# A two-layer hybrid decoder step: the same instructions, ordered by another model of the engines

## The chip, the cores and the metric

The kernel runs on one core of a Trainium2 chip. Its engines work side by side, each from a queue of its own that is fixed when the program is built: TensorE (PE in the profile) multiplies matrices, VectorE (DVE), ScalarE (ACT) and GpSimd (POOL) do the element-wise work, and SyncE (SP) starts most of the transfers. The metric is the device time of one execution in microseconds (us), the median of several runs.

## The reference

One inference step of a decoder trunk with two layers, for 288 tokens: a new sequence of 256 and 8 sequences of 4 sample tokens with states that are carried on. Each layer feeds x to one wide input projection; its columns go to three token mixers, and the results are merged by gates:

```python
proj = jnp.einsum('btd,de->bte', x, w_in)
(a_qkv, a_z, a_beta, a_decay, r_q, r_k, r_v, r_g,
 m_q, m_k, m_v, m_o, m_i, m_f, gates) = jnp.split(proj, split_at, axis=-1)
...
# A gated DeltaNet (causal conv, chunked triangular solve), B retention, C mLSTM
...
x = LN(alpha * x + mix)
x = LN(alpha * x + squared_relu_mlp(x))
```

D_MODEL is 1024, the MLP's inner width 4096, each mixer has four heads of 128. The mixers' states, old and new, are read and written.

## The kernel before, in words

Tokens lie along the free dimension (288 columns), features along the partitions, in 8 slices of 128. All weights are streamed once, in blocks of 512 KB (`wr`, 4 buffers), in the order of SyncE's queue. As products are taken in a split form of fp32, ScalarE rounds each block to a high part (L358, `wh` or `bh`) and VectorE subtracts it for the low part (L360, `wl` or `bl`). One output tile of 128 features is 24 matmuls: for each of 8 slices high by XH, high by XL, low by XH (L367 to L369; L375 to L377 where three tiles go side by side; L504 where a "filler" issues them in pieces between other work). XH and XL are the high and low part of x, made in the same way.

A layer goes through these stages. Convolution and gates: the projections of the DeltaNet come first, VectorE runs the short convolution (L610), and a chain of small 4-row operations makes the gates' sums (L646 to L720). It ends in `dr` (L720), which TensorE needs for `dec` (L724). Then comes a block of small TensorE work: `colp` and `cols` (L733 to L751), transposes `tp` (L409), masks `rm` and `rms` (L809 to L819), Gram products G (L844) and KQ (L801, L854). Between its steps the source calls the filler, which issues projections of the retention mixer (rk, rv, rg; tiles `pj`). Retention's output OR is normalised (`finish`, L965 to L975, with an rsqrt of eleven small VectorE steps, L382 to L393) and transposed (L982). Then follow W and the triangular solve, the products with the states (`kSs`, `qSs`, `rcr`, `mcr`, Xs at L1213, which reads R from L1196), the state's updates (GpSimd scales at L937), the projections of the three branches (`pg`, `br`) and `wo`.

LayerNorm (L1290 to L1381) stands behind `wo` and behind the MLP. To gain time it takes the next matrix product over the sums before they are normalised: three tiles `g1` are multiplied by the raw values, and corrected later by mean, rstd and two columns `wgb` (L1376 to L1380, tile `u`). p1 and p2 (L1339, L1340) are the mean and the square sum, as matmuls by ones. VectorE makes mean and variance (L1345 to L1347), y minus mean (L1355), with ScalarE's Ln and Exp rstd (L1349 to L1353), then for each slice y times rstd (L1359); ScalarE makes XH of it (L1361), VectorE or ScalarE XF (L1365 or L1363), VectorE XL = XF - XH (L1367). The first tiles of the MLP, `f1`, need XH and XL of every slice. After the second LayerNorm it is the next layer's `pj`.

The order in each engine's queue is set by the tile layer: it takes the instructions in the source's order, with what they depend on, and a model of the engines by which it decides which ready instruction goes next into which queue. Two helpers tie single instructions to others (`tc.issue_after`, in `paced` and `Stream.get`), and the constants FILL_* and AHEAD_* say how many matmuls the fillers issue and how many blocks are fetched early. Semaphores and the buffers of the pools are put in afterwards.

## Time and profile before

| | us |
| --- | --- |
| median of three runs | 1285.8 (1285.58 to 1287.79) |
| the profiled execution | 1285.11 |
| its span | 1283.3 |
| TensorE busy | 1201.7 (94%) |
| VectorE busy | 909.0 (71%) |
| ScalarE busy | 597.1 (47%) |
| GpSimd busy | 126.6 (10%) |

The granted clock of TensorE was 0.97 on the mean. A share of busy time is a mean over stages that are limited by different things; so each stage is read by its own window, and each wait by what ended it. In the rows, "[4.80 <-DVE dr L720]" means that the engine had been idle for 4.80 us, and that the end of VectorE's instruction of line 720, which wrote `dr`, let it go on. Buffer numbers are left out in names.

### The profile page before, as it was taken

What the parts mean: (1) busy time and instruction counts of PE and PEld (TensorE: products, weight loads), DVE (VectorE), ACT (ScalarE), POOL (GpSimd) and SP (SyncE); (2) the same over time, 40 slices, a digit from 0 to 9 for tenths busy, and PEclk for the clock granted to TensorE, in tenths of its full rate; (3) what the DMA queues carried; (4) which work ended last, traced back from release to release, by engine and by line L of the source; (5) the groups of instructions that cost most, each with busy time, mean ns of one, the idle gap of its engine ahead of it and who ended that gap; (6) DMA issues with size and microseconds to landing.
All of it is one profiled execution on the core that took longest, in us unless ns stands there. A gap on an engine that the chain in (4) does not pass through costs nothing.

```text
span 1283.3 us, 22945 instructions
## 1 busy us (share of the span) xinstructions
PE 1201.7 (94%) x9210; PEld 1169.4 (91%) x9210; DVE 909.0 (71%) x1617; ACT 597.1 (47%) x1006; POOL 126.6 (10%) x107
## 2 busy tenths in 40 slices
PE   9989899889999999999997988998899998999995
PEld 8978799789999899999996987997799998999995
DVE  6988846596558974566899877556856688645665
ACT  5645324433445653455584532453334566534532
POOL 1113400330000000000000413004200000000000
PEclk9989999889999999999998998998899998999998
DMA  8443624348554465555714454253575543655551
GB/s 311 124 146 107 214 85 152 124 181 243 166 167 123 142 181 164 168 168 162 245 57 133 119 176 154 90 182 140 169 211 164 165 156 94 193 166 165 164 165 38
DMA packets 69794, 201.27 MB, mean 157 GB/s; under 512 B 11688, under 2 KB 22232, under 8 KB 69560
## 3 DMA queue, kind: packets, MB, share of 16 engines
q1 hardware_dynamic: 68744, 197.64, 49.1%
q0 software_dynamic: 944, 2.17, 0.5%
q8 instruction: 72, 1.18, 0.4%
q14 instruction: 34, 0.28, 0.1%
HBM read 180.62 MB, written 17.03 MB: 154 GB/s over the span
## 4 chain that ended last, share of the span: by engine, by line
PE 71%; DVE 18%; DMA 4%; ACT 3%; issue 3%; SPq 1%; DVEq 0%; ACTq 0%
PE f L369 9%; PE f L367 9%; PE f L368 9%; PE pj L504 6%; DVE wl L360 5%; PE pg L367 4%; PE pg L368 4%; PE pg L369 4%; PE pj L369 2%; PE pj L368 2%; PE pj L367 2%; PE br L367 2%; PE br L368 2%; PE br L369 2%; DMA wr<-in_w_ff 1%
## 5 line engine op out<-in xcount | busy, mean ns | idle before, releaser
L360 DVE TENSOR_TENSOR wl<-wr,wh 128x1024 fp32r<-128x1024 f32 x292 | 370.8, 1272 | 182.2 <-ACT wh L358 175.3
L358 ACT CAST wh<-wr 128x1024 fp32r<-128x1024 f32 x292 | 306.2, 1050 | 398.6 <-PE f L368 96.0
L369 PE MATMUL f<-fh,wl 128*128 128x288 f32 x512 | 151.2, 295 | 0.0
L367 PE MATMUL f<-fh,wh 128*128 128x288 f32 x512 | 151.1, 295 | 0.0
L368 PE MATMUL f<-fl,wh 128*128 128x288 f32 x512 | 151.0, 295 | 0.0
L369 PE MATMUL f<-XH,wl 128*128 128x288 f32 x416 | 122.5, 295 | 1.3 <-DVE wl L360 1.3
L368 PE MATMUL f<-XL,wh 128*128 128x288 f32 x416 | 123.1, 296 | 0.0
L367 PE MATMUL f<-XH,wh 128*128 128x288 f32 x416 | 122.9, 296 | 0.0
L367 PE MATMUL pg<-XH,wh 128*128 128x288 f32 x384 | 116.6, 304 | 0.0
L368 PE MATMUL pg<-XL,wh 128*128 128x288 f32 x384 | 114.9, 299 | 0.0
L369 PE MATMUL pg<-XH,wl 128*128 128x288 f32 x384 | 114.3, 298 | 0.0
L369 PE MATMUL pj<-XH,wl 128*128 128x288 f32 x352 | 107.2, 306 | 6.6 <-DVE wl L360 6.6
L367 PE MATMUL pj<-XH,wh 128*128 128x288 f32 x352 | 106.9, 304 | 1.7 <-ACT CV L596 1.7
L368 PE MATMUL pj<-XL,wh 128*128 128x288 f32 x352 | 106.1, 302 | 0.0
L504 PE MATMUL pj<-XH,wh 128*128 128x288 f32 x320 | 99.9, 312 | 0.0
L504 PE MATMUL pj<-XL,wh 128*128 128x288 f32 x320 | 98.1, 306 | 0.0
L504 PE MATMUL pj<-XH,wl 128*128 128x288 f32 x320 | 97.8, 306 | 0.0
L369 PEld LDWEIGHTS f<-fh,wl 128*128 128x128 f32 x512 | 96.3, 188 | 0.1
L367 PEld LDWEIGHTS f<-fh,wh 128*128 128x128 f32 x512 | 96.2, 188 | 0.2
L368 PEld LDWEIGHTS f<-fl,wh 128*128 128x128 f32 x512 | 96.2, 188 | 0.1
L369 PEld LDWEIGHTS f<-XH,wl 128*128 128x128 f32 x416 | 78.4, 189 | 1.8 <-DVE wl L360 1.7
L367 PEld LDWEIGHTS f<-XH,wh 128*128 128x128 f32 x416 | 78.6, 189 | 0.0
(508 smaller groups left out, 2887.9 us busy)
## 6 DMA issues: line engine op xcount, KB each, us to landing
wr<-in_w_in SPq DMA_DIRECT2D x141, 512.0 KB
wr<-in_w_ff SPq DMA_DIRECT2D x128, 512.0 KB
wr<-in_w_out SPq DMA_DIRECT2D x16, 512.0 KB
S<-in_state_ml_C SPq DMA_DIRECT2D x8, 516.0 KB
S<-in_state_ret_R SPq DMA_DIRECT2D x8, 512.0 KB
out_s_R<-S SPq DMA_DIRECT2D x8, 512.0 KB
S<-in_state_dn_S SPq DMA_DIRECT2D x8, 512.0 KB
out_s_S<-S SPq DMA_DIRECT2D x8, 512.0 KB
```

The costliest lines, as they stand in the source:

```text
L358: S.copy(hi[:, k, :], r[:, k, :])
L360: V.tensor_tensor(lo[:, k, :], r[:, k, :], hi[:, k, :].bitcast(F32), op=ALU.subtract)
L367: PE.matmul(ps, hi[:, k, :], xh[k], start=start and k == 0, stop=False)
L368: PE.matmul(ps, hi[:, k, :], xl[k], start=False, stop=False)
L369: PE.matmul(ps, lo[:, k, :], xh[k], start=False, stop=stop and k == KT - 1)
L504: ins = PE.matmul(self.ps[:, :T], self.w[i // 2][:, k, :], (xh, xl, xh)[i][k], start=self.k == 0, stop=self.k == 23)
```

## The change

One argument is added where the program is built. With it the tile layer orders the instructions by a simulation of the engines' timeline in place of its default model. The source of the computation, the pools and the constants are the same, and so are the instructions: 8574 matmuls, 447 transfers and four loads of activation tables in both.

```diff
-    with tile.TileContext(nc) as tc:
+    with tile.TileContext(nc, schedule_with_timeline_sim=True) as tc:
         tile_trunk(tc, a)
```

What moves is the order in the queues, in both layers alike. Three places follow; the numbers in names tell tiles apart.

TensorE's queue around `dec` in layer 1, before. `dec`, `colp` and `cols` stand between matmuls of the filler for rk (`pj_912`):

```order
L504 MATMUL pj_912<-XH_85,wh_908 128x288
L504 MATMUL pj_912<-XL_86,wh_908 128x288
L724 MATMUL dec_869<-dr_845,ones 128x64
L733 MATMUL colp_883<-ident,RS_72_649 128x128 x2
L733 MATMUL colp_883<-ident,RS_73_650 128x128 x2
L743 MATMUL cols_899<-ident,rep_900 128x128
L504 MATMUL pj_912<-XH_85,wl_909 128x288
L504 MATMUL pj_912<-XH_85,wh_908 128x288
```

The same place after; `pj_1247` is the last tile of rv, CO are the convolved values, and `csd` their sample columns:

```order
L504 MATMUL pj_1247<-XH_85,wl_1244 128x288
L724 MATMUL dec_869<-dr_845,ones 128x64
L733 MATMUL colp_883<-ident,RS_72_649 128x128 x2
L733 MATMUL colp_883<-ident,RS_73_650 128x128 x2
L743 MATMUL cols_899<-ident,rep_900 128x128
L409 MATMUL tp_983<-ident,CO_362 128x128 x4
L409 MATMUL tp_989<-ident,CO_362 128x128 x4
L409 MATMUL tp_995<-ident,csd_38_382 128x128
L409 MATMUL tp_1055<-ident,CO_461 128x128 x4
L743 MATMUL cols_899<-ident,rep_903 128x128
```

All tiles of rk and rv have moved ahead of `dec`, which goes from row 429 of TensorE's queue to row 556, and the block behind it stands without projection matmuls up to G.

VectorE's queue in the LayerNorm after `wo` of layer 1, before; `yo` is y, `wl_4887` a split of a weight block, and `u_4855` the correction of the first g1 tile:

```order
L360 TENSOR_TENSOR wl_4887<-wr_4884,wh_4886 128x1024
L1352 TENSOR_TENSOR rstd_4812<-rstd_4812,Cb_4382 128x288
L1376 COPY wgb_4853<-g_750_4731 128x2
L1353 SCALAR_TENSOR_TENSOR rstd_4812<-rstd_4812,Cb_4382 128x288
L1378 SCALAR_TENSOR_TENSOR u_4855<-sd_4383,wgb_4853,g_750_4731 128x288
L1359 TENSOR_TENSOR yo_4380<-yo_4380,rstd_4812 128x288 x2
L1365 TENSOR_SCALAR XF_4820<-yo_4380,vec 128x288 x2
L1367 TENSOR_TENSOR XL_4459<-XF_4820,XH_4458 128x288 x2
```

And after:

```order
L1378 SCALAR_TENSOR_TENSOR u_4867<-sd_4383,wgb_4865,g_752_4733 128x288
L1352 TENSOR_TENSOR rstd_4812<-rstd_4812,Cb_4382 128x288
L1353 SCALAR_TENSOR_TENSOR rstd_4812<-rstd_4812,Cb_4382 128x288
L360 TENSOR_TENSOR wl_4998<-wr_4995,wh_4997 128x1024
L360 TENSOR_TENSOR wl_5034<-wr_5031,wh_5033 128x1024
L1359 TENSOR_TENSOR yo_4380<-yo_4380,rstd_4812 128x288 x4
L1359 TENSOR_TENSOR yo_4381<-yo_4381,rstd_4812 128x288 x4
L1379 TENSOR_TENSOR u_4855<-u_4855,rstd_4812 128x288
L1379 TENSOR_TENSOR u_4861<-u_4861,rstd_4812 128x288
L1379 TENSOR_TENSOR u_4867<-u_4867,rstd_4812 128x288
L1365 TENSOR_SCALAR XF_4820<-yo_4380,vec 128x288 x3
L1365 TENSOR_SCALAR XF_4820<-yo_4381,vec 128x288 x2
```

The eight L1367 (XL) stand behind these rows, where before the first two of them came after two L1359. On TensorE p1 and p2 of this LayerNorm have moved as well, to the end of the g1 tiles:

```order
L376 MATMUL g_752_4733<-XL_4459,bh_4715 128x290
L377 MATMUL g_752_4733<-XH_4458,bl_4716 128x290
L1339 MATMUL p_728_4659<-sd_4383,ones 128x288
L1340 MATMUL p_729_4660<-sqs_4384,ones 128x288
L375 MATMUL f_777_4890<-XH_4458,bh_4721 128x288
L375 MATMUL f_778_4891<-XH_4458,bh_4727 128x288
```

Before, 48 matmuls of g1 stood between p2 and f. In the LayerNorm between the layers L1352 and L1353 moved behind the `wgb` and L1378 of the g1 tiles, and again all of L1359 ahead of the first XL.

VectorE's queue ahead of OR in layer 1, before, where `fr` is the result of the rsqrt, and two splits stand between its steps and the multiply:

```order
L360 TENSOR_TENSOR wl_1902<-wr_1899,wh_1901 128x1024
L392 TENSOR_TENSOR rsu_262_1736<-rsu_262_1736,rst_261_1727 128x8
L548 SCALAR_TENSOR_TENSOR ZG_1718<-ZG_1718,pj_1792 128x288
L393 SCALAR_TENSOR_TENSOR fr_259_1725<-rsu_262_1736,rsy_260_1726 128x8
L386 TENSOR_SCALAR rst_283_1871<-rst_283_1871 128x1
L360 TENSOR_TENSOR wl_1976<-wr_1973,wh_1975 128x1024
L974 TENSOR_SCALAR fr_259_1725<-fr_259_1725 128x8
L387 TENSOR_TENSOR rsy_282_1870<-rsy_282_1870,rst_283_1871 128x1
L975 TENSOR_TENSOR OR_1477<-OR_1477,fr_259_1725 128x1024
```

And after:

```order
L392 TENSOR_TENSOR rsu_262_1736<-rsu_262_1736,rst_261_1727 128x8
L393 SCALAR_TENSOR_TENSOR fr_259_1725<-rsu_262_1736,rsy_260_1726 128x8
L974 TENSOR_SCALAR fr_259_1725<-fr_259_1725 128x8
L948 SCALAR_TENSOR_TENSOR S_1551<-S_1551,up_1668 128x2x128 x2
L1045 TENSOR_TENSOR OR_1477<-smp_1581,ros_1583 128x128
L975 TENSOR_TENSOR OR_1477<-OR_1477,fr_259_1725 128x1024
L948 SCALAR_TENSOR_TENSOR S_1561<-S_1561,up_1707 128x2x128 x2
L948 SCALAR_TENSOR_TENSOR S_1561<-S_1561,up_1712 128x2x128 x2
L360 TENSOR_TENSOR wl_1822<-wr_1819,wh_1821 128x1024
```

The splits that stood ahead of OR now stand behind it.

## Rows read from the trace of the kernel before

**Rows 1.** The page's first part: busy us, share of the span and instructions of TensorE with its weight loads, and of VectorE with ScalarE and GpSimd.

```profile
PE 1201.7 (94%) x9210; PEld 1169.4 (91%) x9210; DVE 909.0 (71%) x1617; ACT 597.1 (47%) x1006; POOL 126.6 (10%) x107
```

**Rows 2.** TensorE's waits over the span, put together by what it waited for: us in total, times, the longest.

```profile
PE tp L982 <- DVE OR L975: 11.4, 2, 5.8
PE Xs L1213 <- DVE R L1196: 10.0, 2, 5.0
PE dec L724 <- DVE dr L720: 7.9, 2, 4.8
PE pj L369 <- DVE wl L360: 6.6, 3, 5.1
PE f L375 <- ACT XH L1361: 5.5, 2, 3.5
```

**Rows 3.** Windows (us from the span's start): length, busy us (and instructions) of PE, PE's weight loads, DVE, ACT and POOL, granted clock, share of the DMA engines, GB/s.

```profile
40.00:68.00 28.00, 25.65 (x189) 24.95 (x188) 27.54 (x50) 16.82 (x32) 4.18 (x5) 1.00 0.51 152
68.00:80.00 12.00, 7.20 (x44) 6.97 (x43) 11.28 (x28) 2.64 (x6) 2.74 (x2) 0.80 0.56 155
80.00:112.00 32.00, 30.53 (x236) 30.03 (x235) 28.13 (x59) 16.71 (x40) 10.64 (x4) 0.97 0.34 97
150.00:180.00 30.00, 23.61 (x181) 23.14 (x180) 19.67 (x46) 8.02 (x12) 3.44 (x2) 0.94 0.37 122
676.00:700.00 24.00, 16.82 (x113) 16.13 (x111) 23.35 (x49) 9.20 (x18) 1.48 (x4) 0.86 0.36 115
780.00:806.00 26.00, 20.34 (x146) 19.91 (x144) 17.31 (x46) 7.01 (x11) 2.23 (x2) 0.87 0.35 112
...
78.00:82.00 4.00, 4.00 (x19) 4.00 (x18) 2.87 (x7) 1.34 (x2) 0.00 (x0) 0.50 0.50 150
```

**Rows 4.** VectorE's timeline ahead of `dr` and ahead of OR in layer 1: start, duration, line, operation, out<-in.

```profile
72.13 1.22 DVE L360 TENSOR_TENSOR wl<-wr,wh 128x1024 fp32r<-128x1024 f32 x1
73.38 2.85 DVE L706 TENSOR_TENSOR RB<-rc,RB 4x288 fp32r<-4x288 f32 x2
...
158.71 1.20 DVE L360 TENSOR_TENSOR wl<-wr,wh 128x1024 fp32r<-128x1024 f32 x1
160.03 1.22 DVE L975 TENSOR_TENSOR OR<-OR,fr 128x1024 f32<-128x1024 f32 x1
```

**Rows 5.** The same window of 80 to 112 us: TensorE's matmuls of line 504 alone (busy us and count, then its weight loads), VectorE's splits of line 360 alone, and from VectorE's timeline and its groups by line the short L392, and the rotary products of rk and rq (busy us, mean ns).

```profile
80.00:112.00 32.00, 22.19 (x142) 20.01 (x140) 0.97 0.34 97
...
80.00:112.00 32.00, 7.27 (x6) 0.97 0.34 97
...
101.58 2.19 DVE L392 TENSOR_TENSOR rsu<-rsu,rst 128x9 f32<-128x9 f32 x1
...
L578 DVE TENSOR_TENSOR rk<-rk,rot 128x1152 f32<-128x1152 f32 x1 | 3.3, 3252 | 0.0
...
L578 DVE TENSOR_TENSOR rq<-rq,rot 128x1152 f32<-128x1152 f32 x1 | 1.4, 1360 | 0.0
```

**Rows 6.** TensorE's timeline in the LayerNorm after `wo` of layer 1.

```profile
428.44 0.65 PE L1340 MATMUL p<-sqs,ones 128*128 128x288 f32 x2
...
435.24 0.30 PE L377 MATMUL g<-XH,bl 128*128 128x290 f32 x1
437.47 0.53 PE L375 MATMUL f<-XH,bh 128*128 128x288 f32 x2 [1.93 <-ACT XH L1361]
```

**Rows 7.** VectorE's timeline in the same place.

```profile
433.51 0.46 DVE L1351 SCALAR_TENSOR_TENSOR rstd<-Cb,sqs 128x288 f32<-128x288 f32 x1 [0.35 <-ACT Cb L1350]
433.88 1.22 DVE L360 TENSOR_TENSOR wl<-wr,wh 128x1024 fp32r<-128x1024 f32 x1
435.02 0.45 DVE L1352 TENSOR_TENSOR rstd<-rstd,Cb 128x288 f32<-128x288 f32 x1
...
435.88 0.51 DVE L1378 SCALAR_TENSOR_TENSOR u<-sd,wgb,g 128x288 f32<-128x288 f32 x1
436.30 0.82 DVE L1359 TENSOR_TENSOR yo<-yo,rstd 128x288 f32<-128x288 f32 x2
437.04 0.76 DVE L1365 TENSOR_SCALAR XF<-yo,vec 128x288 f32<-128x288 f32 x2
437.72 0.82 DVE L1367 TENSOR_TENSOR XL<-XF,XH 128x288 fp32r<-128x288 f32 x2
```

**Rows 8.** The same LayerNorm in layer 2: VectorE's L1351, and TensorE's first rows of f.

```profile
1065.57 0.46 DVE L1351 SCALAR_TENSOR_TENSOR rstd<-Cb,sqs 128x288 f32<-128x288 f32 x1 [1.93 <-ACT Cb L1350]
...
1069.53 0.85 PE L375 MATMUL f<-XH,bh 128*128 128x288 f32 x2 [3.55 <-ACT XH L1361]
1070.18 0.44 PE L375 MATMUL f<-XH,wh 128*128 128x288 f32 x1
```

**Rows 9.** The LayerNorm between the layers: VectorE's last step of rstd, and TensorE's first matmuls of the next layer.

```profile
642.13 0.46 DVE L1353 SCALAR_TENSOR_TENSOR rstd<-rstd,Cb 128x288 f32<-128x288 f32 x1
...
645.32 0.29 PE L375 MATMUL pj<-XH,bh 128*128 128x288 f32 x1
645.45 0.29 PE L376 MATMUL pj<-XL,bh 128*128 128x288 f32 x1
```

**Rows 10.** GpSimd's and VectorE's timelines ahead of Xs in layer 1.

```profile
242.69 7.45 POOL L937 TENSOR_TENSOR S<-S,DEC 128x1024 f32<-128x1024 f32 x4
...
244.95 6.28 DVE L360 TENSOR_TENSOR wl<-wr,wh 128x1024 fp32r<-128x1024 f32 x1 [3.17 <-PE pj L369]
```

## The prediction

> **What bounds the kernel now.** I read the page first: TensorE (PE) is busy 1201.7 of 1283.3 us and VectorE (DVE) 909.0, so the whole is TensorE's, and 81.6 us at most lie in its waits, head and tail [rows 1]. The times of before are 1285.8 us (median of three); the profiled execution took 1285.11 us, 0.7 us less, with a span of 1283.3, so about 1.8 us lie around the span. Sums below go on 1285.11. The second view, TensorE's waits put together by what they wait for, says that its long waits are few and come in pairs, one per layer, and that nearly all end on VectorE: the retention output OR (11.4 us), the state product at Xs (10.0), `dr` ahead of `dec` (7.9), a weight split wl (6.6), and XH in the LayerNorm after `wo` (5.5) [rows 2]. VectorE is not full, but it works its queue in order; a wait there is a matter of what stands ahead of the step that TensorE wants. The windows, third, show the stretches where that bites, and that a long wait costs twice: the granted clock is 0.80 over 68 to 80 us, and still 0.50 in 78 to 82 [rows 3]. That is half speed, and 12 x 0.20 + 2 x 0.5 = 3.4 us are lost to it after the 4.8 us wait for `dr`.
>
> The change adds and removes no instruction. What moves is each engine's queue, so every term below is one of waits: which are no longer there, and which are new. In the long stretches of br, ff and f2, where TensorE waits for next to nothing, the order is the same as far as I compared it.
>
> **Terms that get shorter: the front of the mixers.** Before, VectorE placed a 1.22 us split and the two 4-row subtractions L706 (2.85 us) ahead of dr, and two splits, of 1.2 us each by the one shown, between the rsqrt steps and the OR multiply [rows 4]. After, TensorE gets the tiles of rk and rv in one piece before `dec`, so dr has 127 more matmuls ahead of it, some 17 us at 0.13 each [rows 9]; and OR stands ahead of the splits. By that, these go in layer 1: 2.35 us idle in 40 to 68, 4.80 in 68 to 80 with its 3.4 of half clock, the OR wait of 5.8 with the 0.06 x 30 = 1.8 of half clock in 150 to 180 [rows 2, 3]: 18.1. In layer 2: 24 - 16.8 = 7.2 idle and 0.14 x 24 = 3.4 of clock in 676 to 700, 26 - 20.3 = 5.7 idle and 0.13 x 26 = 3.4 of clock in 780 to 806 [rows 3]: 19.7. Together 37.8 us, the upper end.
>
> What is late next is the dense block. From `dec` to KQs TensorE now has transposes, masks and Gram products back to back, without the projection matmuls between them. In 80 to 112 us those matmuls (L504) were 22.19 of TensorE's 30.53 busy us, so its own share is 8.3 us; VectorE was busy 28.13 there, less 7.27 in splits and about 7.4 in the four long rotary operations, of which the costliest two are shown: some 13.5 [rows 3, 5]. If the two run side by side TensorE waits 13.5 - 8.3 = 5 us per layer, if they strictly take turns 13.5. I take 8, nearer to the lower end since ScalarE too clears transposes; per pair of layers 16. The lower end of the whole front term is 37.8 - 27 = 11, and 6 with a half clock in the block; my value is 37.8 - 16 = 21.8.
>
> A rule speaks against even that. The short L392 (128x9) took 2.19 us and the rotary product of rk 3.25 us where that of rq took 1.36 [rows 5], each while GpSimd ran a tensor operation. The Trainium skill (SBUF — State Buffer, "SBUF: two separate sides") says that VectorE and GpSimd share a port pair as a lock, so that an operation with two SBUF inputs blocks until the other engine's is through; the trace agrees. GpSimd's operations in the block keep their order, and by that rule, with two such waits of about 2 us more falling into the block, the front term would be 21.8 - 8 = 14; I leave it out of the sum, since before paid it too.
>
> **Terms that get longer: LayerNorm after `wo`, both layers.** Before, p1 and p2 (mean and square sum) go to TensorE ahead of seven eighths of the g1 matmuls; those run from the end of p2 at 428.44 + 0.65 = 429.09 to 435.5, while VectorE makes rstd and the first yo, XF, XL; f waits 1.93 us [rows 6]. After, p1 and p2 come behind all of g1, directly ahead of f: the cover of 6.4 us is gone. VectorE's order also grows: before, wl, L1352, wgb, L1353, one L1378, then two yo, two XF, two XL in turn. After, all three L1378, two wl, all eight yo (L1359), three L1379, five XF (L1365), and only then the first XL, which the sixth matmul of f needs. Worked out from p2's end with the starts of the rows, which give 0.37 us per L1351, L1352, L1353, L1359 and L1379, 0.34 per L1365, 0.42 per L1378, 1.14 per wl [rows 7]: to L1351 433.51 - 429.09 = 4.42; then 0.37 + 3 x 0.42 + 2 x 0.37 + 2 x 1.14 = 4.65; 8 x 0.37 = 2.96; 3 x 0.37 = 1.11; 5 x 0.34 = 1.70; the first XL 0.45: 15.3 us, in which f has five matmuls, 0.7 us. 14.6 idle against 1.93 is +12.7; bounds 8 (one XL early enough to matter, a faster start of rstd) and 14. In layer 2 f waited 3.55 us, because L1351 stood 1.93 us for ScalarE's Exp [rows 8]: +11.0. The half clock follows a wait of that length: in layer 2 f's matmuls already show it, 0.44 us each for 0.30 [rows 8], so only layer 1 pays anew, 3.4. Sum +27.1.
>
> **LayerNorm between the layers, once.** Before, rstd was done at 642.6 and pj followed g1 at 645.32 with no wait [rows 9]. After, L1352 and L1353 stand behind the wgb and L1378 of all three g1 tiles, so rstd ends some 1.7 us (0.1 + 0.4 x 2 + 0.37 and handing over) after the last g1 matmul instead of 2.7 before it. Then 8 x 0.37, one XF 0.34, 3 x 0.37, 4 x 0.34, one XL 0.45: 7.9 us from the end of g1, less five matmuls and the eight gate matmuls (1.7): +6.2, and 3.4 of half clock, +9.6. Bounds 2 and 13.
>
> **Small ones.** Xs waits 5.0 us per layer for R, which sits behind a split that took 6.28 us while GpSimd scaled the state from 242.69 on [rows 10]; four more matmuls stand ahead of Xs and 0.7 us of VectorE's order: -1 each, -2. The tail's partial p1 and p2 move behind the last tile: within 1 us, 0. Loads of the DeltaNet state move behind a weight block in SyncE's queue: 0, up to +3 per layer.
>
> **Sum.** 27.1 + 9.6 - 21.8 - 2 = +12.9: 1285.1 + 12.9 = 1298; I say 1297, a little towards the lower bounds of the two LayerNorm terms.
>
> **Rivals.**
> (B) The front wins. The dense block hides its waits beside ScalarE and the rk and rv tiles, so the whole 37.8 goes; the LayerNorms cost their lower ends (8 + 7 + 2, with one half clock 20). 1285.1 - 37.8 - 2 + 20 = 1265; with half of each change, 1276. For it: VectorE has the room, and six of the named waits sit there. Against: VectorE is busy 27.54 of 28 and 23.35 of 24 us just ahead of two of them [rows 3].
> (C) The dense block decides, on the slow side: it becomes turn-taking between TensorE and VectorE in both layers, 13.5 us each, and TensorE falls to half clock in it, on which its own 8.3 us take some 5.5 more: 19 us per layer, from where the front's gain is nil: 1285.1 + 36.7 - 2 = 1320. For it: the block has no cover left; against: ScalarE and the PSUM buffers let several steps stand open.
> (D) The order makes no difference, since waits just move within a layer and TensorE's sum of work stays: 1285. Against it is the lost cover in the LayerNorms, which nothing behind can give back.
>
> **How the numbers follow.** Forecast 0.60, B 0.22, C 0.12, D 0.06. The likeliest case's own range is 1288 to 1308. For 8 in 10 I go down into B to 1270 and up to 1316, just short of C. A change under 0.2% (2.6 us) can't be told from none: faster 0.25 (B and a little of the forecast's lower side), same 0.07, slower 0.68.
>
> **What would show it.** Right: new waits of TensorE at f for XL of 10 us or more around each LayerNorm after `wo` and of 6 at pj between the layers, half clock behind them, no wait left at `dec` and OR, and short waits at tp, rm and G instead. Wrong: f waiting under 5 us; or `dec` to KQs longer than before, against which the moved tiles don't count; or OR's wait still there.

## The result, and the profile after

The changed kernel took 1299.5 us (median of four runs, 1298.39 to 1301.83) against 1286.8 for the kernel before in the same comparison. The ratio is 1.010, with an interval of 1.008 to 1.012: slower by about 13 us. The forecast was 1297, slower, with a likeliest range of 1288 to 1308. The profiled execution took 1300.14 us.

The page's first part, after; it answers to [rows 1]:

```profile
PE 1204.4 (93%) x9210; PEld 1174.8 (90%) x9210; DVE 896.9 (69%) x1617; ACT 591.8 (46%) x1006; POOL 125.0 (10%) x107
```

The counts are the same. TensorE is busy 2.7 us longer with the same matmuls, and its span is 1298.4 for 1283.3, so some 12 of the 15 us are idle time. (Some of the program's matmuls, p1 and p2 among them, stand as two rows in the trace, so that it counts more than the 8574 of the program.) TensorE's waits put together, after (us in total, times, the longest); they answer to [rows 2]:

```profile
PE f L375 <- ACT XH L1361: 21.1, 2, 10.6
PE rm L809 <- DVE R L788: 10.3, 2, 6.7
PE pg L367 <- ACT tg L1257: 9.9, 2, 5.0
PE dec L724 <- DVE dr L720: 8.2, 2, 5.7
PE f L376 <- DVE XL L1367: 7.8, 2, 3.9
PE wo L367 <- DVE yo L1316: 4.4, 2, 2.2
PE Xs L1213 <- DVE R L1196: 4.2, 2, 2.3
...
PE pj L375 <- ACT XH L1361: 3.1, 1, 3.1
```

Read the two lists side by side. The waits for OR (11.4) and wl (6.6) are gone, and Xs fell from 10.0 to 4.2. New are f for XH and XL, 28.9 together where 5.5 stood, rm for R, pg for tg, and pj for XH. The wait for `dr` is still there: 8.2 against 7.9.

Waits alone don't say where the time went, since a wait can be paid earlier or later. So I take TensorE's timeline at places that have the same work ahead of them. First the kernel before (start, duration, line, operation):

```profile
76.59 0.69 PE L724 MATMUL dec<-dr,ones 128*128 128x64 f32 x2 [4.80 <-DVE dr L720]
111.94 0.38 PE L854 MATMUL KQs<-csd,csd 128*128 128x128 f32 x2
163.07 1.52 PE L801 MATMUL W<-Q,E 128*128 128x128 f32 x8
306.30 0.40 PE L367 MATMUL br<-OH,wh 128*128 128x288 f32 x1
395.61 0.29 PE L375 MATMUL wo<-mh,wh 128*128 128x288 f32 x1
480.47 0.30 PE L367 MATMUL f<-fh,wh 128*128 128x288 f32 x1
...
937.39 0.40 PE L367 MATMUL br<-OH,wh 128*128 128x288 f32 x1
1026.83 0.29 PE L375 MATMUL wo<-mh,wh 128*128 128x288 f32 x1
1114.49 0.30 PE L367 MATMUL f<-fh,wh 128*128 128x288 f32 x1
```

And after:

```profile
90.32 0.69 PE L724 MATMUL dec<-dr,ones 128*128 128x64 f32 x2 [2.50 <-DVE dr L720]
117.47 0.38 PE L854 MATMUL KQs<-csd,csd 128*128 128x128 f32 x2
158.10 1.06 PE L801 MATMUL W<-Q,E 128*128 128x128 f32 x8
296.68 0.29 PE L367 MATMUL br<-OH,wh 128*128 128x288 f32 x1
388.10 0.29 PE L375 MATMUL wo<-mh,wh 128*128 128x288 f32 x1
487.44 0.30 PE L367 MATMUL f<-fh,wh 128*128 128x288 f32 x1
...
938.98 0.30 PE L367 MATMUL br<-OH,wh 128*128 128x288 f32 x1
1030.37 0.29 PE L375 MATMUL wo<-mh,wh 128*128 128x288 f32 x1
1128.61 0.30 PE L367 MATMUL f<-fh,wh 128*128 128x288 f32 x1
```

The differences of these starts, stage by stage, beside what the prediction's terms give for the same stage:

| stage | measured us | predicted us |
| --- | --- | --- |
| start to br, layer 1 | -9.6 | -11.1 |
| br to wo | +2.1 | 0 |
| wo to the second half of the MLP (LayerNorm after `wo`) | +14.5 | +16.1 |
| from there to br of layer 2 (LayerNorm between the layers, front) | -5.4 | 9.6 - 12.7 = -3.1 |
| br to wo, layer 2 | +1.9 | 0 |
| wo to the second half of the MLP, layer 2 | +10.6 | +11.0 |
| the rest | +0.9 | 0 |
| sum | +15.0 | +12.9 |

The front's predicted values are 18.1 - 8 and 19.7 - 8, each with 1 us more for Xs. (The sum is of the two profiled executions; the medians differ by 13.)

The LayerNorm after `wo` first. Windows after (length, busy us and instructions of PE, PE's weight loads, DVE, ACT and POOL, granted clock, share of DMA, GB/s) in layer 1, of a stretch of which [rows 3] shows none:

```profile
425.00:440.00 15.00, 4.43 (x29) 3.87 (x28) 10.26 (x20) 2.27 (x5) 0.00 (x0) 0.82 0.11 36
440.00:446.00 6.00, 2.11 (x8) 1.76 (x8) 6.00 (x18) 6.00 (x13) 0.00 (x0) 0.50 0.35 119
```

In 425 to 446 TensorE works 6.5 of 21 us. Its timeline there, which answers to [rows 6], has p2 as the last work before the gap:

```profile
428.49 0.65 PE L1340 MATMUL p<-sqs,ones 128*128 128x288 f32 x2
439.71 0.85 PE L375 MATMUL f<-XH,bh 128*128 128x288 f32 x2 [10.57 <-ACT XH L1361]
...
445.17 0.61 PE L376 MATMUL f<-XL,bh 128*128 128x288 f32 x1 [3.89 <-DVE XL L1367]
```

And VectorE's, which answers to [rows 7]:

```profile
433.76 0.46 DVE L1351 SCALAR_TENSOR_TENSOR rstd<-Cb,sqs 128x288 f32<-128x288 f32 x1 [1.04 <-ACT Cb L1350]
434.13 1.36 DVE L1378 SCALAR_TENSOR_TENSOR u<-sd,wgb,g 128x288 f32<-128x288 f32 x3
...
436.27 2.35 DVE L360 TENSOR_TENSOR wl<-wr,wh 128x1024 fp32r<-128x1024 f32 x2
438.54 3.03 DVE L1359 TENSOR_TENSOR yo<-yo,rstd 128x288 f32<-128x288 f32 x8
```

From p2's end at 429.1 to L1351 it is 4.6 us, then three L1378, two splits, and eight yo before any XF. That is the chain that the prediction had added up, row by row. In layer 2 the same two waits are 10.56 and 3.89.

The second place is `dr`. VectorE's timeline ahead of it, after; it answers to [rows 4]:

```profile
71.57 1.36 DVE L576 TENSOR_TENSOR rq<-rq,cst 128x1152 f32<-128x1152 f32 x1 [0.69 <-DMA rot<-rq]
72.84 2.34 DVE L666 TENSOR_SCALAR U<-U,sc 128x288 f32<-128x288 f32 x1
...
89.98 0.29 DVE L720 TENSOR_TENSOR dr<-cst,drv 128x32 f32<-128x32 f32 x2
```

dr comes 13.7 us later than before. The gate chain that ends in it (L666 is one of its steps) now runs among the rotary products of rq and five splits more: 27 stand ahead of dr, 22 did. Two experiments below test whether that is why. The 127 matmuls that moved ahead of `dec` are 17.1 us of work at 0.135 each, and `dec` starts 13.7 us later: 3.4 us of them are gain, no more. What follows shows in the window from `dec` to KQs, of all engines and then of the filler's matmuls (line 504) alone. First before:

```profile
76.59:111.94 35.35, 33.88 (x249) 33.38 (x249) 31.11 (x67) 16.84 (x40) 10.64 (x4) 0.92 0.34 95
...
76.59:111.94 35.35, 24.13 (x148) 0.92 0.34 95
```

And after:

```profile
90.32:117.47 27.15, 23.21 (x121) 22.37 (x122) 23.71 (x60) 10.03 (x31) 8.44 (x4) 0.63 0.36 102
...
90.32:117.47 27.15, 4.14 (x21) 0.63 0.36 102
```

With 127 matmuls less the stretch is 8.2 us shorter, not 17.1: 8.9 are lost in it. Idle time in it grew from 1.5 to 3.9 us; the clock took 0.08 x 35.35 = 2.8 before and takes 0.37 x 27.15 = 10.0 now.

These marks are of one execution each, and such marks spread. Four kernels of the experiments below have the changed kernel's rows in the queues of TensorE, VectorE, ScalarE and GpSimd up to 266 us or further, and two have those of the kernel before up to 157 us. Over the five executions with the new order `dec` starts at 89.1 to 90.3 us, KQs at 113.4 to 117.5 and W at 156.0 to 165.6; over the three with the old order `dec` starts at 76.6 to 78.8 and KQs at 111.9 to 113.8. So the gain at `dec` is 3.4 to 6.9 us and the loss from there to KQs 6 to 9, and the two traces shown lie at the unfavourable end: KQs is 5.5 us later in them, and 2.3 us later on the mean of all eight.

The third is pg, a wait that the prediction didn't have. ScalarE's timeline in layer 1, after:

```profile
266.77 1.04 ACT L964 ACTIVATE sq<-OM 128x1024 f32<-128x1024 f32 x1
269.09 1.02 ACT L1257 ACTIVATE tg<-pg 128x288 f32<-128x288 f32 x3 [1.29 <-DVE fss L965]
```

The tanh of pg (`tg`) frees the PSUM tile that TensorE wants next. It stands behind the square of OM, a step of the mLSTM's normalisation (`finish`), and TensorE waits 4.97 us for it, in both layers.

### The profile page after: what moved, and what is told of

It reads as the page before. It is cut to its first block, busy times and chain, and to the rows that moved or that the text cites. A ratio compares the mean times of both kernels' runs of the same rounds, so it can differ in the third digit from the quotient of the medians.

```text
span 1298.4 us, 22933 instructions
## 1 busy us (share of the span) xinstructions
PE 1204.4 (93%) x9210; PEld 1174.8 (90%) x9210; DVE 896.9 (69%) x1617; ACT 591.8 (46%) x1006; POOL 125.0 (10%) x107
## 3 DMA queue, kind: packets, MB, share of 16 engines
q0 software_dynamic: 944, 2.17, 0.5%
## 4 chain that ended last, share of the span: by engine, by line
PE 83%; DVE 10%; DMA 3%; issue 2%; ACT 1%; SPq 0%; DVEq 0%; ACTq 0%
PE f L368 10%; PE f L369 9%; PE f L367 9%; PE pj L504 5%; PE pg L369 4%; PE pg L368 4%; PE pg L367 4%; PE pj L368 4%; PE pj L369 4%; PE pj L367 4%; DVE wl L360 2%; PE br L369 2%; PE br L367 2%; PE br L368 2%; PE up L943 1%
## 5 line engine op out<-in xcount | busy, mean ns | idle before, releaser
L360 DVE TENSOR_TENSOR wl<-wr,wh 128x1024 fp32r<-128x1024 f32 x292 | 364.9, 1252 | 208.4 <-ACT wh L358 207.3
L358 ACT CAST wh<-wr 128x1024 fp32r<-128x1024 f32 x292 | 305.9, 1049 | 429.1 <-PE f L368 94.4
L368 PE MATMUL pj<-XL,wh 128*128 128x288 f32 x352 | 104.6, 297 | 0.0
L367 PE MATMUL pj<-XH,wh 128*128 128x288 f32 x352 | 104.4, 297 | 0.0
L369 PE MATMUL pj<-XH,wl 128*128 128x288 f32 x352 | 104.0, 297 | 0.0
L504 PE MATMUL pj<-XH,wh 128*128 128x288 f32 x320 | 97.4, 304 | 0.0
L504 PE MATMUL pj<-XL,wh 128*128 128x288 f32 x320 | 96.9, 303 | 0.0
L504 PE MATMUL pj<-XH,wl 128*128 128x288 f32 x320 | 96.4, 302 | 0.2 <-DVE wl L360 0.2
L367 PEld LDWEIGHTS pg<-XH,wh 128*128 128x128 f32 x384 | 75.0, 195 | 10.9 <-ACT tg L1257 10.4
```

Source lines behind the costliest of these rows:

```text
L358: S.copy(hi[:, k, :], r[:, k, :])
L360: V.tensor_tensor(lo[:, k, :], r[:, k, :], hi[:, k, :].bitcast(F32), op=ALU.subtract)
L367: PE.matmul(ps, hi[:, k, :], xh[k], start=start and k == 0, stop=False)
L368: PE.matmul(ps, hi[:, k, :], xl[k], start=False, stop=False)
L369: PE.matmul(ps, lo[:, k, :], xh[k], start=False, stop=stop and k == KT - 1)
L504: ins = PE.matmul(self.ps[:, :T], self.w[i // 2][:, k, :], (xh, xl, xh)[i][k], start=self.k == 0, stop=self.k == 23)
```

## The experiments

Each kernel is compared with the kernel before, timed beside it on the same chip. Since the median of before was 1282.1 to 1287.6 in different comparisons, kernels are compared here by their ratios; 0.0010 is 1.3 us. The expectations are in us, each counted from a median measured earlier. The theory was that the LayerNorm after `wo` costs more than the whole loss, in two parts (VectorE's order, p's place), and that the front gives back less than its waits suggest. The rival was that the block behind `dec` decides.

**VectorE's order in the LayerNorms.** From the changed kernel: yo of slice f may go only after XL of slice f - 2.

```diff
...
-                V.tensor_tensor(y, y, rstd, op=ALU.mult)
+                with nullcontext() if f < 2 or last else tc.issue_after(done[f - 2].ins):
+                    V.tensor_tensor(y, y, rstd, op=ALU.mult)
...
-                V.tensor_tensor(u_, u_, rstd, op=ALU.mult)
+                with tc.issue_after(done[5].ins):
+                    V.tensor_tensor(u_, u_, rstd, op=ALU.mult)
```

> The changed order, with one pin: in each LayerNorm that feeds a product, the multiply by rstd of slice f (from slice 2 on) and the three u*rstd come behind the XL of slice f-2 (and of slice 5) in VectorE's queue, so XL of slice 0 follows two multiplies and two XF instead of eight and five. p1 and p2 stay at the end of g1. Theory (VectorE's order and the lost cover are two separate parts of the cost): the second wait at f (for XL, 3.9 us per layer) goes, the first (for XH, 10.6) stays as it is, since the first multiply starts no earlier: 1299.5 - 8 = 1291, 1288 to 1296. Rival (all of the cost is VectorE's order): both waits fall to some 3 us, 1270. Rival (what is saved here is waited for elsewhere): 1299, within 2.

Measured: 1291.7 us, ratio 1.0033 (1.0013 to 1.0052), 0.7% below the change's 1.0100. The wait for XL is gone; that for XH stays at 10.6. So this part of the order costs some 8.6 us, as expected.

**p's place.** From the changed kernel: seven eighths of g1 may go only after p2, as before.

```diff
-                PE.matmul(p2[:, :T], ones, sq_, start=True, stop=True)
+                p2_ins = PE.matmul(p2[:, :T], ones, sq_, start=True, stop=True)
             if not last:
-                mm3_group(p_t, nxt, xh, xl, range(1, 8))
+                with tc.issue_after(p2_ins.ins):
+                    mm3_group(p_t, nxt, xh, xl, range(1, 8))
```

> The changed order, with the other pin: the g1 matmuls from the second slice on come behind p2 in TensorE's queue, so that 63 of them cover VectorE's chain. VectorE's pins of the first experiment are not in. Theory: from the end of p2 XL of slice 0 comes after 4.4 + 1.1 (rstd) + 2.3 (two wl) + 3.0 (eight multiplies) + 1.7 (five XF) + 0.8 = 13.3 us, of which 63 matmuls cover 8.4 and five of f 0.7: a wait of some 4 us in all for 14.5, so 10 us less per layer; with the half clock behind the long wait 3 more per layer; and the LayerNorm between the layers loses its waits of 3.1 and 1.3: 1299.5 - 26 - 5 = 1269, 1264 to 1282. Rival (cover isn't what was lost): over 1292.

Measured: 1285.6 us, ratio 1.0008 (0.9989 to 1.0028). This one edit takes the loss away, but it gives 12 us and not the 30 that were expected, and lies outside the expected range. TensorE's timeline in the LayerNorm of layer 1 says why:

```profile
417.87 0.40 PE L375 MATMUL g<-XH,bh 128*128 128x290 f32 x1 [2.42 <-DVE yo L1316]
421.61 1.33 PE L1339 MATMUL p<-sd,ones 128*128 128x288 f32 x2 [2.87 <-DVE sd L1320]
...
437.54 0.40 PE L376 MATMUL f<-XL,bh 128*128 128x288 f32 x1 [3.89 <-DVE XL L1368]
```

The 10.6 us for XH are gone. But p now waits 2.87 us for the sums `sd`, and the matmuls of g1 that could run meanwhile are queued behind it. A pin that restores the cover behind p takes away the cover ahead of it.

**Both.** The two edits together.

> Both pins together. Theory: XL of slice 0 is there 4.4 + 1.1 + 2.3 + 0.7 + 0.7 + 0.6 = 9.8 us behind p2, under a cover of 9.1: waits of under 2 us at f in both layers, none between the layers, no half clock there. That gives back the stage's cost of 14.5 and 10.6 us against before and some 5 between the layers: 1299.5 - 30 = 1269, 1262 to 1275, faster than before. Rival (front and LayerNorm aren't independent, what is saved in the LayerNorms is waited for behind them): 1285 or more.

Measured: 1280.8 us, ratio 0.9968 (0.9943 to 0.9993). With both LayerNorm edits the new order is faster than the kernel before, by about 4 us: they give back about 17 us (1.0100 to 0.9968). 30 were expected, and the upper end of the expected range was 1275. What is missing is in the LayerNorms too: the stage from wo to the second half of the MLP is still 5.0 us longer than before in layer 1 and 2.1 in layer 2, which fits the waits of g and p that it keeps (2.42 and 2.68 in each layer). So 17 us is less than the whole cost of the LayerNorms, and what the new order gains elsewhere is more than 4 us, by these numbers an estimated 11.

**The other way: p behind g1, in the kernel before.** This is the mirror image. p1 and p2 of the LayerNorm after `wo` go behind all of g1; VectorE's order is left to follow.

```diff
...
-                mm3_group(p_t, nxt, xh, xl, range(1))
+                late = gname == "ln1_g"
+                mm3_group(p_t, nxt, xh, xl, range(8 if late else 1))
+                g_end = g_last[0]
...
+                with tc.issue_after(g_end.ins) if late else nullcontext():
+                    PE.matmul(p1[:, :T], ones, sd, start=True, stop=True)
+                    PE.matmul(p2[:, :T], ones, sq_, start=True, stop=True)
```

> The order of before, with p1 and p2 of the LayerNorm after wo pinned behind all of g1, as the change has them; the other LayerNorms stay. VectorE keeps the default model's interleaving. Theory (the lost cover is a cost of its own): from the end of p2 the first XH comes after 4.4 + 1.1 + 1.3 (u) + 0.4 + 0.6 = 7.8 us, XL before f needs it: f waits 8 us in each layer for 1.9 and 3.5, and in layer 1 the half clock comes behind it, 3.4: 1285.7 + 6 + 4.5 + 3.4 = 1300, 1293 to 1304. Rival (the cost was VectorE's order alone): 1290 or less.

Measured: 1299.0 us, ratio 1.0097 (1.0069 to 1.0125). TensorE's waits put together, of that kernel:

```profile
PE f L377 <- ACT XH L1366: 14.1, 2, 7.0
```

So p's place alone makes the kernel before as slow as the changed one by the ratio. In the profiled execution its two stages are longer by 5.9 and 2.5 us; 3.6 us more lie ahead of br in layer 1. Up to there every engine's queue has the rows of the kernel before, so these 3.6 us are no effect of the order; they are of the size by which single executions spread.

**The tiles of rk and rv ahead of `dec`, in the kernel before.** The filler issues 45 pieces there instead of 3.

```diff
-FILL_C = (3, 3, 2, 3)
+FILL_C = (45, 3, 2, 3)
```

> The order of before (default model), with one constant changed: 45 units of filler (135 matmuls) ahead of dec in place of 3, which puts dec in row 523 of TensorE's queue (before 429, after 556) and leaves the block behind it with less filler; VectorE's queue stays the default model's. It asks what the moved tiles alone are worth. Theory by the chip so far (TensorE's queue as before in the changed kernel made it 9 us slower, but the changed kernel's block stands 5.5 us later at KQs than before's, so the moved tiles only hide that VectorE is later with dr): dec's waits of 4.8 and 3.1 us go, the block's own waits come: 1285.7 + 2 x (8 - 4) = 1294, 1284 to 1302. Rival, my prediction's first term: the waits ahead of dec and their half clock go and little comes back: 1275 or less.

Measured: 1303.5 us, ratio 1.013 (1.0103 to 1.0157), just above the expected range. TensorE's waits put together:

```profile
PE tp L982 <- DVE OR L975: 18.5, 2, 9.2
PE cols L743 <- DVE rep L742: 11.3, 2, 6.4
```

The wait for `dr` is gone, as the prediction's front term wanted, and it is paid again: at `cols`, and at OR, where 11.4 became 18.5. KQs starts at 122.4 us for 111.9, with 39 matmuls more ahead of it (5.3 us); W, with the same matmuls ahead of it, starts at 172.0 for 163.1. VectorE's queue differs too, from 72 us on, so this isn't the effect of TensorE's order alone. The reading that fits is that work which is moved ahead of one wait is missing behind it, where it had hidden the next two.

**OR ahead of the splits, in the kernel before.** Three more weight blocks of the z tiles may be split before the OR multiply, and none of the mq tiles.

```diff
...
+        zfill.st.skip, zfill.st.after = 3, fin_ins[0].ins
+        fill.then.st.after = fin_ins[0].ins
```

> The order of before, with one pin: in both layers the splits of the last z tile and of the mq tiles come behind the multiply that makes OR, so that the two splits of 1.2 us that stood between the rsqrt steps and OR stand behind it; TensorE's queue is row for row that of before. Theory (OR's wait is a matter of what stands ahead of it on VectorE): the wait falls from 5.8 and 5.7 to some 3.4 us, and a part of the half clock behind it with it: 1285.7 - 2 x 2.4 - 1 = 1280, 1277 to 1283. Rival (OR is late because its inputs are): 1285, within 2; or the splits are missed behind it and it is no gain.

Measured: 1281.3 us, ratio 0.9953 (0.9931 to 0.9975). TensorE's wait for OR, in both layers together, which was 11.4:

```profile
PE tp L984 <- DVE OR L977: 6.6, 2, 3.6
```

So OR's place is worth some 6 us in the kernel before. This is the one gain of the change that is shown by itself. In the changed kernel the wait is gone and KQs to W takes 40.6 us where it took 51.1; of the 8.4 us of idle time that it had there 5.8 were OR's. That stretch is less sure than it looks, since it took 40.4 to 50.6 us in the five executions with the new order (the last section has the slowest).

**The block behind `dec` as before.** From the changed kernel: each piece of the filler is tied behind the step that it followed in the source, with constants that place it as before.

```diff
-FILL_C = (3, 3, 2, 3)
-FILL_T = (12, 8, 8)
+FILL_C = (14, 0, 0, 7)
+FILL_T = (2, 8, 8)
...
+            def behind(self, n):
+                with tc.issue_after(pe_out[0].ins):
+                    return self(n)
...
-        fill(FILL_C[1])
+        fill.behind(FILL_C[1])
...
```

> The changed order, but the filler's matmuls from dec to KQs tied behind the block's steps, so that TensorE's queue there has nearly before's order (dec in row 430 for 429). VectorE's queue elsewhere, OR's place and the LayerNorms stay as changed. My prediction's reading (the moved rk and rv tiles give the front's gain): dec waits again and 5 us per layer are lost: 1309. The rival that the trace of the changed kernel now suggests (KQs, with the same matmuls ahead of it, stands 5.5 us later than before, and the gain comes with OR alone): the waits at rm (3.7 and 6.7 us) and the half clock in the block go, dec's wait comes back: 1299.5 - 10 = 1290, 1284 to 1296.

Measured: 1308.4 us, ratio 1.0163 (1.0134 to 1.0192). It was meant to tell what the dense block costs, and it doesn't. The number is that of the prediction's reading, but not by its 5 us per layer: `dec` has its old place in TensorE's queue, and dr comes at 85.6 us, 4.4 earlier than in the changed kernel and 9.3 later than before, so that TensorE waits 15.0 and 16.6 us for it. It shows only that TensorE's old order doesn't fit this order of VectorE, and that undoing one of the two is worse than either.

So the next one also holds VectorE's splits behind dr, but for two:

```diff
...
+        fill.st.skip, fill.st.after = 2, dr_ins.ins
+        fill.then.st.after = dr_ins.ins
```

> As the run with TensorE's block as before (1308.4), and on VectorE all splits of rk and rv from the third on pinned behind dr: 18 splits stand ahead of dr there, where the changed kernel has 24 and before 19. It asks why dec waited 15 and 17 us in that run. Theory (the changed kernel's VectorE order is made for late dec: it has five splits more and the rotary of rq ahead of dr, some 6 + 2.7 us, so TensorE's old order can't use it; the two orders only make sense together): dec's wait falls by 6 x 1.2 = 7 us per layer: 1308.4 - 14 = 1294, 1289 to 1300. Rival (dr is late because of ScalarE or of the convolution): 1306 or more.

Measured: 1307.3 us, ratio 1.0163 (1.0129 to 1.0198); `dec` still waits 12.8 and 15.9 us. By its number that is the rival, but the trace names neither ScalarE nor the convolution. VectorE's timeline of that kernel, with every line number some 7 higher:

```profile
65.86 0.37 DVE L673 TENSOR_SCALAR U<-U,sc 128x288 f32<-128x288 f32 x1
...
69.80 1.36 DVE L583 TENSOR_TENSOR rq<-rq,cst 128x1152 f32<-128x1152 f32 x1 [1.99 <-DMA rot<-rq]
71.19 2.36 DVE L680 TENSOR_TENSOR RS<-IT,CS 4x288 f32<-4x288 f32 x1
...
81.44 0.29 DVE L727 TENSOR_TENSOR dr<-cst,drv 128x32 f32<-128x32 f32 x2
```

The splits weren't all of it. The gate chain stands still for 1.99 us because the rotary of rq, next in the queue, waits for a DMA; then its 4-row step takes 2.36 us. dr is at 81.4, 5 us later than before even without the splits.

**The rotary of rq behind dr.** From the changed kernel alone:

```diff
...
-        rq = rotary(tproj("rq"))
+        rq = tproj("rq")
...
+        with tc.issue_after(dr_ins.ins):
+            rotary(rq)
+            rqs = sample_of(rq, "cs0")
```

> The changed order, with the rotary of rq (two operations of 1.4 us on VectorE, and the copy of its sample columns) traced and pinned behind dr; the LayerNorms as changed. The trace of the changed kernel shows the gate chain in VectorE's queue behind the first of these, which waits for a transfer (the rotated copy of rq), and the next 0.3 us step of the chain taking 2.3 us while GpSimd works on that copy. Theory: dr comes 1.4 + 0.7 + 2.0 + 1.4 = 5.5 us earlier, dec's waits (2.5 and 5.7 us) go, the block starts up to 5 us earlier: 1299.5 - 8 = 1291, 1287 to 1297. Rival (the chain waits for ScalarE or the splits, so dr and the block stay): 1299, within 2.

Measured: 1294.1 us against 1282.1 for before, ratio 1.0084 (1.0053 to 1.0114), about 2 us better than the change, within the intervals, where 8 were expected: the 1294.1 lies in the expected range only because before was faster in this comparison too. In its profiled execution dr moved from 90.0 to 83.2 us (88.7 to 90.0 in the five executions with the new order), some 6 us as expected, so the rotary is a cause of the late dr. KQs moved from 117.5 (113.4 to 117.5) to 112.1. But in layer 1 W starts at 157.4 for 158.1, and br no earlier than in the changed kernel; in layer 2 br comes 6 us earlier. What holds W in layer 1 is in the trace: between KQs and W TensorE is idle for 4.2 us, where it was 0.1, with 1.9 at `stk` and 2.1 in three waits at `rcr` for the transfer of retention's old state. `rcr` starts at 137.7 us there, and at 137.7 to 139.1 in the three executions with the new order that wait at it too. So what KQs gains is waited for at that transfer; why it doesn't land sooner was not found.

**Combinations.** Both LayerNorm edits, and OM's `finish` moved behind the first tanh of pg:

```diff
...
-        fin_mp = finish(OM, dn, MG, None, 2, 0, 8)
...
+                    if j == 1:
+                        with tc.issue_after(tg_ins.ins):
+                            fin_mp = finish(OM, dn, MG, None, 2, 0, 8)
```

> Both LayerNorm pins, and the square of OM's normalisation on ScalarE pinned behind the second gate's tanh (its transposes go two gates on). The traces of the changed kernel and of both pins have a wait of 5.0 us per layer at pg: three PSUM buffers are full, and the tanh that empties them stands behind that square in ScalarE's queue and waits for its buffer. Theory: the two waits go: 1280.8 - 10 = 1271, 1266 to 1276. Rival (tanh is late for another reason, the weight block or the buffer of an older tile): 1280, within 3.

Measured: 1277.4 us, ratio 0.9922 (0.9892 to 0.9952), the lowest ratio of all, 0.8% faster than the kernel before. pg still waits, 2.6 us per layer for 5.0, so about half of the expected 10 us came. The third edit's own share is not sure: its interval touches that of the two LayerNorm edits (0.9943 to 0.9993).

That kernel with the block as before and the splits behind dr:

> Both LayerNorm pins and the late square of OM (1277.4), with the same front: TensorE's block as before and the splits of rk and rv behind dr. Theory: before's front up to KQs had 2.6 us less than this version's (111.9 against 114.5) in layer 1 and some 3 in layer 2, but dr still stands behind the rotary of rq, 2.7 us: 1277.4 - 2 = 1275, 1269 to 1281. Rival (what holds for the last run adds up: the block without cover is better with this VectorE order): 1283 or more.

Measured: 1286.5 us, ratio 0.9992 (0.997 to 1.0014): it gives back the 0.7%, at `dec` (12.8 and 15.7 us), as the rival had it.

And that kernel (LayerNorm edits and OM) with the rotary behind dr instead:

> The fastest version so far (both LayerNorm pins and the late square of OM, 1277.4) with the same rotary pin. Theory: dec's waits there (2.5 and 6.9 us) go, some half clock with them: 1277.4 - 8 = 1269, 1264 to 1274. Rival: 1277, within 2.

Measured: 1274.7 us against 1282.1, ratio 0.9932 (0.9906 to 0.9958): no better than without the rotary's move, where 8 us were expected. dr came 5.5 us earlier in layer 1 here too (84.2 for 89.7), but in the profiled execution TensorE then waited 1.8 us at `stk` and 1.7 for the same transfer, and KQs to W took 51.7 us.

## Why the prediction was right, and where it was not

**LayerNorm after `wo`: right.** Predicted 14.6 idle us in each layer; measured 10.57 + 3.89 and 10.56 + 3.89. The two parts were one number in the prediction and are two causes on the chip. p behind g1 is the larger (12 us when undone, 12 to 13 by the ratio when put into the kernel before, of which that trace shows 8.4 in the two stages), VectorE's order the smaller (8.6). Only the second part has the XL of which the prediction spoke: the first wait of f is for XH, which the prediction's chain passes on its way.

**LayerNorm between the layers: right in kind, too large.** 6.2 idle us were predicted, and TensorE, which had no wait there before [rows 9], waited 3.12 at pj and 1.33 at the gate matmuls. The granted clock in 654 to 666 us, in steps of 4 us, was 0.80, 0.50 and 0.85, so half clock adds 3.4 at most, and it stays under the predicted 9.6; how far can't be told, since the stage's end lies in moved work.

**Xs: as predicted in kind, larger**: 4.2 us of wait remain of 10.0, for -2 predicted [rows 2, 10]. The place paid it back at pg: +9.9, of which the prediction said nothing. I had compared VectorE's queue there and not ScalarE's. The wait of wo for yo (4.4 for 1.7) wasn't foreseen either.

**The front: net about right, by the wrong steps.** Layer 1 gained 9.6 for 11.1; over the executions with the same rows, br starts at 294.3 to 302.7 us in four of the new order, and at 306.3 and 309.9 in two of the old. The step that failed is "By that, these go in layer 1: 2.35 us idle in 40 to 68, 4.80 in 68 to 80 with its 3.4 of half clock". It took dr's own time as given. dr moved by 13.7 us, and the two experiments on it name the splits and rq's rotary in VectorE's queue (with both edits in one kernel it was not tried). So `dec` gained 3.4 us of the 7.15 idle. The 3.4 of half clock didn't go either: the block's cost was 8 in the prediction, 4.6 net of that half clock, and is 8.9. By KQs layer 1 has lost 5.5 us where the sum had 2.5 gained. The error of 8 us was made up behind: to W 10.5 us come back (7.6 predicted), and to br 4.6 more (1 predicted). OR came as predicted, and more. That these errors nearly cancel is luck, and with it that the forecast of 1297 stands so close to 1299.5; where the executions with the same rows are taken together, KQs is 2.3 us late in place of 5.5, and the error is some 5 us.

**The dense block: rival C was half right.** C had 13.5 us of turn-taking and 5.5 of half clock. It is 3.9 idle, most of it one wait of 3.67 for R, and 10.0 of half clock (5 to 10 over the five executions with the new order). The prediction's lower end of 6 for the front had that half clock in one layer; with C's 5.5 in both it is 0. So the block takes the gain up to KQs, but doesn't decide the kernel. Rival D (waits only move) describes what the tiles ahead of `dec` did in the kernel before, but OR ahead of the splits shows that an order can be worth 6 us by itself.

**What would show it.** Of the signs named, the waits at f, the half clock behind them, and OR without a wait came; "no wait left at `dec`" did not. "`dec` to KQs longer than before, against which the moved tiles don't count" was named as a sign of a wrong forecast, and it came, with 8.9 us: for that step it was one.

## What to carry to other kernels

An order of one queue is only good with the orders of the others. Before a moved block of matmuls is counted as cover, follow the instruction that it waits for through its own engine's queue, and look for what stands ahead of it there, above all a step that waits for a DMA; where cover moves, ask which later wait it had hidden. When a scheduler's other model is tried, take its result apart by stages with the same work ahead, and pin the few places that lost: here two pins turned +1.0% into -0.3%, and with a third it was -0.8%. Before a few us at one mark are given a cause, look for executions with the same rows up to that mark, and see how far they spread: here it was up to 10 us.

## What the runs showed of the hardware that was not expected

**A busy TensorE at half clock.** A window of the changed kernel, columns as above:

```profile
102.00:114.00 12.00, 12.00 (x57) 11.64 (x57) 11.66 (x22) 5.84 (x22) 6.32 (x3) 0.51 0.00 0
```

After the 3.67 us wait for R the clock stays at the lower of its two levels (0.50 of 2.4 GHz is 1.2) for nearly all of 12 us while the engine is counted busy without a gap, with masks, transposes and Gram products; in 114 to 117, with projection matmuls, it is 1.00. Behind the waits of f in the LayerNorm, with the matmuls of f, it was back sooner: 0.96 in 448 to 450, where the last wait ended at 445.2. I had priced a half clock as a fixed 3.4 us per long wait; from `dec` to KQs it cost 10.0.

Whether it falls differs between executions of the same rows. In the kernel with VectorE's order pinned, whose queues are those of the changed kernel up to 439 us, TensorE waited 1.25 and 0.58 us at `rcr`, between 137 and 141, for the transfer of retention's old state, and 0.50 followed; in the changed kernel it had no such wait. That kernel's window first, then the changed kernel's:

```profile
142.00:156.00 14.00, 14.00 (x78) 11.44 (x77) 8.65 (x22) 1.93 (x4) 7.18 (x3) 0.50 0.53 176
...
142.00:156.00 14.00, 13.92 (x112) 12.36 (x105) 12.57 (x30) 4.64 (x8) 6.57 (x3) 1.00 0.75 248
```

KQs to W took 50.6 us there for 40.6. The kernel with the LayerNorm edits and the late OM waited 1.28, 0.54 and 0.56 us at the same place and kept 1.00; what decides it, these traces don't show.

**A short VectorE step that takes six times as long.** `U<-U,sc` took 0.37 us where GpSimd was idle (65.86 in the kernel with the splits behind dr) and 2.34 us in the changed kernel, where GpSimd ran this:

```profile
71.64 3.38 POOL L577 TENSOR_TENSOR rot<-rot,cst 128x1152 f32<-128x1152 f32 x1 [14.81 <-DMA rot<-rq]
```

That ends at 75.0, and the step at 75.2. The Trainium skill (SBUF — State Buffer, "SBUF: two separate sides") has VectorE's operations in a two-port mode, or with two SBUF inputs, wait until GpSimd's instruction is through, if that started first; the trace agrees in the starts (71.64 and 72.84) and in the ends, though which of the two cases this step is, no run shows. Two inputs aren't needed for it: in the kernel with rq's rotary behind dr a copy with one input, `IT<-GT`, took 2.17 us beside GpSimd's same step, and 0.30 in the changed kernel. So an order that puts a chain's steps beside GpSimd's work makes the chain itself longer, which a count of the instructions ahead of dr doesn't tell.
